# Moving five small norm tiles and 32 bytes in a 20,000-instruction transformer kernel, so that the big operands share one offset modulo 512 bytes

## The chip, the core and the metric

The kernel runs on one core of a Trainium2 chip. A core has TensorE (PE in the rows; PEld is its weight load), VectorE (DVE), ScalarE (ACT), GpSimd (POOL) and SyncE (SP, which issues most of the DMAs here). They share the on-chip memory SBUF, 128 partitions wide; TensorE writes its products into PSUM. Every tile below is 128 partitions high, and its address means the byte in each partition. The metric is the device time of one execution in microseconds (us); a time for a kernel is the median of several executions.

## What is computed

Two transformer blocks over 512 tokens of width 1024, in fp32. Cut to its skeleton:

```python
# first block (one layer)
x = x + rms_norm(hybrid_mixer(rms_norm(x), ...))            # sparse attention + matrix memory
x = x + rms_norm(memory_cross_attention(rms_norm(x), ...))
x = x + rms_norm((silu(h @ w_gate) * (h @ w_up)) @ w_down)  # h = rms_norm(x), d_ff 2816
# second block (two layers): half feed-forward, convolution module, half feed-forward,
# then half feed-forward, stick-breaking attention, half feed-forward
x = x + 0.5 * ((silu(h @ w_gate) * (h @ w_up)) @ w_down)    # four times
```

All norms are `x * rsqrt(mean(x*x) + eps) * gain`. Nearly all work is `activations @ weights`: five feed-forward modules of 1024 x 2816 x 3, and some twenty 1024-wide projections.

## The kernel before

Activations lie feature-major: a tile holds 128 features of all 512 tokens, 2 KB in each partition. fp32 accuracy comes from a split: `split` (lines 121 to 133) makes of a tile its rounded part `hi` (on ACT) and the remainder `lo` (on DVE), and `load_w` (line 159) does the same with a slab of weights, 128 x 1024, which SP's DMA queue has brought to `wraw`. `mm3` (lines 169 to 172) then adds three products, each a weight load and a matmul of 128 x 128 stationary by 128 x 512 moving:

```python
nc.tensor.matmul(ps, lh, rh, start=start, stop=False)   # L170: whi, xh
nc.tensor.matmul(ps, lh, rl, start=False, stop=False)   # L171: whi, xl
nc.tensor.matmul(ps, ll, rh, start=False, stop=stop)    # L172: wlo, xh
```

The stationary operand is a slice of 128 columns (512 bytes) of a weight slab, the moving one an activation tile. `projs` (line 195) walks the 8 K tiles of a projection, `ffn` (line 303) does each feed-forward module in two halves: in a half 11 F tiles, each a gate and an up projection from the activations `xh`, `xl` (11 x 2 x 24 = 528 matmuls), then 8 output tiles, each the down projection from the 11 tiles `hh`, `hl` (8 x 33 = 264 matmuls). `linear_out` (line 379) does an output projection from a module's result (`oh`, `ol` in the cross attention), and in the convolution module the second projection reads `ch`, `cl`, which have the tags and so the places of `xh`, `xl`. `token_tiles` (line 586) swaps the parts: there the activations are stationary and 256 columns of weights move.

The order on each engine comes from the framework's scheduler, except where a region is held in program order (`order_pe`). Weight slabs turn in three buffers of `wraw`, four of `whi` and four of `wlo`; a load waits for a free `wraw`, ACT's split for a free `whi`.

A norm takes the per-token sum of squares by matmuls with a column of ones, and then works on tiny tiles of 4 columns (16 bytes): `ms` (two buffers, line 257) and `rt` (three buffers, line 261), from which `rms_rows` (line 265) spreads the result over the partitions.

Where the tiles lie follows from the pools. Tiles of a pool stand one behind the other, each rounded up to 32 bytes, and the pools on the left side follow each other: `const`, `act_p`, `wp`, then those of the modules. `act_p` holds x, the 16 tiles `xh`, `xl`, four tiles for the squares, then the five small ones (5 x 32 = 160 bytes), then `rb`. In the program as built this gives:

```
tile                                  place                modulo 512
x, xh*, xl*, sq, sqacc, sqlast        from byte 20032          64
ms x2, rt x3                          77376 to 77535     (32 bytes each)
rb                                    77536                   224
wraw, whi, wlo                        from 81632              224
oh/ol, hh/hl, y, vsh, ksh             left side, later        224
cross attention qx*, k*               right side              224
cross attention pTh/pTl, vh/vl        right side              480
sparse attention kz, qn, P            right side               96
```

Of the kernel before, what the change touches and what calls it, by code (L numbers as in the profile page):

```python
# [14 lines left out]
P = 128  # L15
S = 512
# [32 lines left out]
def kernel(ctx: ExitStack, tc: tile.TileContext, t: dict, out: bass.AP):  # L49
# [34 lines left out]
    nhalf = const.tile([P, 4], F32, name="nhalf")  # L84
    nc.gpsimd.memset(nhalf, -0.5)
    nc.scalar.activation(const.tile([P, 4], F32, name="warm0"), nhalf, AF.Copy)
# [48 lines left out]
    # heads of 64: the exact product of queries and keys in two passes, (q_hi + q_lo) (k_hi + k_lo), with the  # L135
    # parts of the keys on the two halves of the partitions and each part of the queries on both
# [16 lines left out]
    def head_scores(ps, q, k, i):  # L153
        """scores of query tile i with its keys, the first 128 (i + 1)"""
        n = max((i + 1) * P, 256)
        for c in range(2):
            nc.tensor.matmul(ps[:, :n], q[c][:, i * P : (i + 1) * P], k[:, :n], start=c == 0, stop=c == 1)

    def load_w(ap, width, raw=None, pieces=1, hp=1):
        """a slab of weights as its rounded part and the remainder"""  # L160
        if raw is None:
            raw = wp.tile([P, width], F32, tag="wraw", bufs=3, name=nm("wraw"))
            nc.sync.dma_start(raw, ap)
        hi = wp.tile([P, width], F32R, tag="whi", bufs=4, name=nm("whi"))
        lo = wp.tile([P, width], F32R, tag="wlo", bufs=4, name=nm("wlo"))
        split(raw, hi, lo, pieces=pieces, hp=hp)
        return hi, lo
# [6 lines left out]
    # steps of a latency chain, put between the products of a run that TensorE takes in program order  # L174
# [27 lines left out]
    def square_acc(src, j, state, ts=WHOLE, apart=False, eng=nc.gpsimd):  # L202
        """adds a tile's squares to the running sum; the last tile's may stay apart"""
        if j == KT - 1 and apart:
            if "last" not in state:
                state["last"] = act_p.tile([P, S], F32, tag="sqlast", name=nm("sqlast"))
            nc.scalar.activation(state["last"][:, ts], src[:, ts], AF.Square)
            return
        sq = act_p.tile([P, S], F32, tag="sq", bufs=2, name=nm("sq"))
        nc.scalar.activation(sq[:, ts], src[:, ts], AF.Square)  # L210
        if j == 0:
            state["first"] = sq
        elif j == 1:
            state["acc"] = act_p.tile([P, S], F32, tag="sqacc", name=nm("sqacc"))
            eng.tensor_tensor(state["acc"][:, ts], state["first"][:, ts], sq[:, ts], ALU.add)  # L215
        else:
            eng.tensor_tensor(state["acc"][:, ts], state["acc"][:, ts], sq[:, ts], ALU.add)

    def inv_rms(state, eps=1e-6, ts=WHOLE, psum_only=False):
        """(mean of squares + eps)^-1/2 per token: as a column per token tile, and as a row on all partitions"""  # L220
        if not state:
            for j in range(KT):
                square_acc(x[j], j, state, eng=nc.vector)
        sums = rms_sums(state, eps, ts)
        rt, pb = rms_rows(sums, ts)
        if psum_only:
            return rt, pb
        rb = act_p.tile([P, S], F32, tag="rb", bufs=2, name=nm("rb"))[:, : ts.stop - ts.start]
        nc.vector.tensor_copy(rb, pb)
        return rt, rb  # L230

    def inv_rms_chain(state, first, second):
        """the steps of inv_rms, after that many products each; the result is there when they are done"""
        if not state:
            for j in range(KT):
                square_acc(x[j], j, state, eng=nc.vector)
        got = []

        def finish():
            rt, pb = rms_rows(got[0], WHOLE)  # L240
            rb = act_p.tile([P, S], F32, tag="rb", bufs=2, name=nm("rb"))
            nc.vector.tensor_copy(rb, pb)
            got[:] = [rt, rb]

        chain.append([first, lambda: got.append(rms_sums(state, 1e-6, WHOLE))])
        chain.append([second, finish])
        return got

    def rms_sums(state, eps, ts):
        n = (ts.stop - ts.start) // P  # L250
        pr = at_tile()
        accs = [state[k] for k in ("acc", "last") if k in state]
        for a, acc in enumerate(accs):
            for i in range(n):
                c = ts.start + i * P
                nc.tensor.matmul(pr[:, 4 * a + i : 4 * a + i + 1], acc[:, c : c + P], ones[:, 0:1], start=True, stop=True)
        ms = act_p.tile([P, 4], F32, tag="ms", bufs=2, name=nm("ms"))
        nc.vector.tensor_scalar(ms[:, :n], pr[:, :n], 1.0 / D, eps, ALU.mult, ALU.add)
        if len(accs) == 2:
            nc.vector.scalar_tensor_tensor(ms[:, :n], pr[:, 4 : 4 + n], 1.0 / D, ms[:, :n], ALU.mult, ALU.add)  # L260
        rt = act_p.tile([P, 4], F32, tag="rt", bufs=3, name=nm("rt"))
        nc.gpsimd.tensor_tensor(rt[:, :n], ms[:, :n], nhalf[:, :n], ALU.pow)
        return rt
# [14 lines left out]
    def post_norm_add(y, state, nxt):  # L278
        """x += y * rb, where y carries its gain already; a step for each half of the tokens"""
# [23 lines left out]
    def ffn(fp, xs, st, wg, wu, wd, out_cb, head=0, tail=0, step=None):  # L303
        """head: F tiles whose projections start with the first half of the tokens; tail: output tiles that end so"""
# [91 lines left out]
    # =====================================================================  # L396
    # hybrid mixer
    # =====================================================================
# [32 lines left out]
    # relative bias: u[h, i] = bias_h(511 - i), masked distances NEG; T[q, c] = -u[127 - q + c]  # L431
# [32 lines left out]
    # gate rows: 0..23 branch gates, 32..35 input gate, 64..67 forget gate  # L464
# [23 lines left out]
    # compressed keys and values  # L488
# [61 lines left out]
    # cumulative gates of the matrix-memory heads  # L550
# [28 lines left out]
    # branch gates, token-major  # L579
# [6 lines left out]
    def token_tiles(chunks, wd, xs_, ntok, cb, ws=None):  # L586
        """out[tokens, wd] for each token tile; chunks hold 1024 / wd K tiles of wd columns"""
# [26 lines left out]
    def coef(sums, h, br, floor):  # L614
        """gate over the sum of the exponentials, per token"""
# [7 lines left out]
    def softmax_rows(ps, bias, ptile, sm, masked):  # L623
        """ps holds the negated scores; writes exp(score - max) to ptile and its row sums to sm"""
# [165 lines left out]
    for hp in range(2):  # L790
# [19 lines left out]
        for i in range(NT):  # L810
# [12 lines left out]
            # num / d, normalized: num * (mean(num^2) + eps d^2)^-1/2 with d = max(|den|, exp(-m))  # L823
# [64 lines left out]
    # =====================================================================  # L888
    # memory cross attention
    # =====================================================================  # L890
# [87 lines left out]
    # P: projection of a feature tile, Q: its query, S, V: a head's scores and values  # L978
# [21 lines left out]
    # =====================================================================  # L1000
    # feed-forward of the first block
    # =====================================================================
# [18 lines left out]
    # =====================================================================  # L1021
    # second block
    # =====================================================================
# [26 lines left out]
    # Depthwise taps on TensorE: 32 channels x 4 taps fill the rows, a diagonal per tap the columns,  # L1050
    # and four such column tiles run side by side; the other taps run on VectorE.
# [45 lines left out]
    def depthwise(j, sets, gl, R, wbd, ts=WHOLE):  # L1097
# [6 lines left out]
        # two independent chains of multiply-adds on VectorE  # L1104
# [17 lines left out]
    def ln_sums(ts):  # L1122
        """mean and variance per token"""
# [31 lines left out]
    def ln_finish(n, lm, m2, ts):  # L1155
        """SiLU of the normalized tiles"""
# [108 lines left out]
    def stick_scores(q, k):  # L1265
        Ws = []
        for i in range(NT):
# [6 lines left out]
            # diagonal block: masked scores  # L1274
# [112 lines left out]
def _tile_cols(w):  # L1387
    """[K, N] -> [N / 128][128 rows of a K tile][K tile][128 columns]"""
# [4 lines left out]
def _tile_rows(w, per):  # L1393
    """[K, N] -> [chunk][128][per K tiles][N]"""
# [4 lines left out]
def _quarters(w):  # L1399
    """groups of 256 columns, each [chunk][128][4 K tiles][256]"""  # L1400
    return np.stack([_tile_rows(w[:, g : g + 256], 4) for g in range(0, w.shape[1], 256)])
# [111 lines left out]
```

## Time and profile before

| what | value |
|---|---|
| three executions | 2839.34 us median (2836.4 to 2841.1) |
| the profiled execution | span 2837.0 us from first to last instruction; its whole time is not listed apart |
| TensorE busy | 2777.5 us, 98% of the span |
| VectorE, ScalarE, GpSimd busy | 52%, 38%, 12% |
| DMA | 263.19 MB, mean 93 GB/s |
| granted TensorE clock | 0.991 of full speed, mean |

In the timeline a matmul's row gives its start and its duration; the durations overlap, since the next matmul enters while the last drains, so the distance from start to start is what a matmul costs TensorE. A form such as `128*128 128x512` is stationary size, then partitions and columns of the moving operand.

### The profile page before, as it was taken

The numbers are of one execution on the slowest core, as the hardware profiler recorded it, in microseconds if no ns is written. First come the engines' busy times: TensorE is split into PE (matmuls) and PEld (weight loads), VectorE is DVE, ScalarE is ACT, GpSimd is POOL, SyncE is SP. The second block draws the span as 40 slices with busy tenths as digits, with TensorE's granted clock in tenths as the row PEclk, the third lists the DMA queues.
The fourth block names the chain that finished last, engine by engine and source line by source line (L and its number), as shares of the span: only waits on it lengthen the run. The fifth ranks groups of instructions, "written<-read, shape, count | busy, mean of one in ns | idle before, by whom it ended". The sixth has DMA issues, their size and how long they took to land.

```text
span 2837.0 us, 35182 instructions
## 1 busy us (share of the span) xinstructions
PE 2777.5 (98%) x13750; PEld 2258.7 (80%) x13750; DVE 1465.4 (52%) x2270; ACT 1075.0 (38%) x1772; POOL 337.9 (12%) x451
## 2 busy tenths in 40 slices
PE   9999999999999999999899999999999997999998
PEld 6877988888888888885688888898888874788887
DVE  7666474643436434449754344434434489543443
ACT  6775544423234222332332233342222366322223
POOL 0133132100002000012210000100000136200001
PEclk9999999999999999999999999999999999999999
DMA  5213321223222232236232322322232310222322
GB/s 199 96 46 105 112 75 58 92 77 109 95 84 90 87 105 96 80 113 171 76 104 86 108 90 83 110 84 101 80 108 87 105 66 3 82 95 84 106 81 81
DMA packets 86923, 263.19 MB, mean 93 GB/s; under 512 B 9655, under 2 KB 13751, under 8 KB 86756
## 3 DMA queue, kind: packets, MB, share of 16 engines
q1 hardware_dynamic: 85148, 258.42, 27.7%
q10 hardware_dynamic: 1608, 2.52, 0.3%
q8 instruction: 108, 1.77, 0.2%
q14 instruction: 59, 0.48, 0.1%
HBM read 256.60 MB, written 4.30 MB: 92 GB/s over the span
## 4 chain that ended last, share of the span: by engine, by line
PE 79%; DVE 4%; DMA 1%; issue 1%; ACT 1%; POOL 0%; SPq 0%; DVEq 0%; ACTq 0%
PE sc L172 9%; PE sc L170 9%; PE sc L171 9%; PE mm L172 7%; PE mm L171 7%; PE mm L170 7%; PE tr L172 6%; PE tr L171 6%; PE tr L170 6%; PE po L172 3%; PE po L170 3%; PE po L171 3%; DVE rm L1280 1%; DVE wlo L130 1%; PE sc L1101 1%
## 5 line engine op out<-in xcount | busy, mean ns | idle before, releaser
L126 ACT ACTIVATE whi<-wraw 128x1024 fp32r<-128x1024 f32 (+3 forms) x518 | 492.2, 955 | 1327.0 <-PE sc L171 458.2
L130 DVE TENSOR_TENSOR wlo<-wraw,whi 128x1024 fp32r<-128x1024 f32 (+4 forms) x559 | 581.6, 1049 | 388.3 <-ACT whi L126 387.4
L170 PE MATMUL mm<-xh,whi 128*128 128x512 f32 (+1 forms) x760 | 291.5, 384 | 5.7 <-ACT whi L126 5.7
L171 PE MATMUL mm<-xl,whi 128*128 128x512 f32 (+1 forms) x760 | 290.5, 382 | 5.5 <-DVE xl L133 5.5
L172 PE MATMUL mm<-xh,wlo 128*128 128x512 f32 (+1 forms) x760 | 291.7, 384 | 0.0
L172 PE MATMUL sc<-xh,wlo 128*128 128x512 f32 (+1 forms) x696 | 274.4, 394 | 0.0
L170 PE MATMUL sc<-xh,whi 128*128 128x512 f32 (+1 forms) x696 | 273.3, 393 | 0.0
L171 PE MATMUL sc<-xl,whi 128*128 128x512 f32 (+1 forms) x696 | 272.6, 392 | 0.0
L171 PE MATMUL tr<-xl,whi 128*128 128x512 f32 (+1 forms) x592 | 226.0, 382 | 2.0 <-DVE xl L133 2.0
L172 PE MATMUL tr<-xh,wlo 128*128 128x512 f32 (+1 forms) x592 | 227.1, 384 | 0.0
L170 PE MATMUL tr<-xh,whi 128*128 128x512 f32 (+1 forms) x592 | 226.2, 382 | 0.0
L215 POOL TENSOR_TENSOR sqacc<-sq,sq 128x512 f32<-128x512 f32 (+1 forms) x11 | 16.4, 1487 | 1618.6 <-issue 915.6
L316 DVE TENSOR_TENSOR su<-sc,rb 128x512 f32<-128x512 f32 x80 | 55.2, 691 | 265.2 <-PE sc L172 265.2
L171 PEld LDWEIGHTS mm<-xl,whi 128*128 128x128 f32 x760 | 144.9, 191 | 35.8 <-DVE xl L133 6.9
L170 PEld LDWEIGHTS mm<-xh,whi 128*128 128x128 f32 x760 | 144.8, 191 | 35.3 <-ACT whi L126 5.7
L172 PEld LDWEIGHTS mm<-xh,wlo 128*128 128x128 f32 x760 | 145.3, 191 | 28.4 <-DVE wlo L130 0.3
L170 PEld LDWEIGHTS sc<-xh,whi 128*128 128x128 f32 x696 | 130.7, 188 | 33.5 <-issue 3.4
L171 PEld LDWEIGHTS sc<-xl,whi 128*128 128x128 f32 x696 | 130.7, 188 | 31.5
L172 PEld LDWEIGHTS sc<-xh,wlo 128*128 128x128 f32 x696 | 130.7, 188 | 30.4
L171 PEld LDWEIGHTS tr<-xl,whi 128*128 128x128 f32 x592 | 112.3, 190 | 26.1 <-DVE xl L133 2.2
L170 PE MATMUL sc<-hh,whi 128*128 128x512 f32 (+1 forms) x352 | 132.6, 377 | 0.0
L171 PE MATMUL sc<-hl,whi 128*128 128x512 f32 (+1 forms) x352 | 132.3, 376 | 0.0
(531 smaller groups left out, 5583.3 us busy)
## 6 DMA issues: line engine op xcount, KB each, us to landing
wraw<-wg SPq DMA_DIRECT2D x110, 512.0 KB, 3.5
wraw<-wu SPq DMA_DIRECT2D x110, 512.0 KB, 3.4
wraw<-wd SPq DMA_DIRECT2D x80, 384.0 KB, 3.0
wraw<-wd SPq DMA_DIRECT2D x80, 320.0 KB, 2.8
wraw<-w_pw SPq DMA_DIRECT2D x24, 512.0 KB, 3.6
wraw<-w_in_f SPq DMA_DIRECT2D x15, 512.0 KB, 4.3
R<-glscr SPq DMA_DIRECT2D x28, 264.0 KB, 5.5
x<-xT SPq DMA_DIRECT2D x16, 256.0 KB, 4.7
```

Of the source, the lines that this page charges most:

```text
L126: last_hi[0] = nc.scalar.activation(hi[:, sl], src[:, sl], AF.Copy)
L130: nc.vector.tensor_tensor(lo[:, sl], src[:, sl], f32(hi[:, sl]), ALU.subtract)
L170: nc.tensor.matmul(ps, lh, rh, start=start, stop=False)
L171: nc.tensor.matmul(ps, lh, rl, start=False, stop=False)
L172: nc.tensor.matmul(ps, ll, rh, start=False, stop=stop)
L215: eng.tensor_tensor(state["acc"][:, ts], state["first"][:, ts], sq[:, ts], ALU.add)
L316: nc.vector.tensor_tensor(su, pu, rb, ALU.mult)
L1101: nc.tensor.matmul(pc[32 * cg : 32 * cg + 32, ts], wbd[:, 4 * g + cg], R[:, cg, 4 * g + ts.start : 4 * g + ts.stop], start=g == 0, stop=g ...
L1280: nc.vector.tensor_tensor_scan(rm[:, :L][:, ::-1], ob[:, 1 : L + 1][:, ::-1], ob[:, 1 : L + 1][:, ::-1], 1.0, ALU.mult, ALU.bypass)
```

## The change

Beside comments and docstrings, which go (all lines from 87 on have moved by at most one), three tiles are touched. `ms` and `rt` are taken from the pool `const` in place of `act_p`, and the tile `warm0`, written once at the start, gets 16 columns in place of 4, of which the same 4 are written:

```diff
     nhalf = const.tile([P, 4], F32, name="nhalf")
     nc.gpsimd.memset(nhalf, -0.5)
-    nc.scalar.activation(const.tile([P, 4], F32, name="warm0"), nhalf, AF.Copy)
+    warm0 = const.tile([P, 16], F32, name="warm0")
+    nc.scalar.activation(warm0[:, :4], nhalf, AF.Copy)
...
-        ms = act_p.tile([P, 4], F32, tag="ms", bufs=2, name=nm("ms"))
+        ms = const.tile([P, 4], F32, tag="ms", bufs=2, name=nm("ms"))
...
-        rt = act_p.tile([P, 4], F32, tag="rt", bufs=3, name=nm("rt"))
+        rt = const.tile([P, 4], F32, tag="rt", bufs=3, name=nm("rt"))
```

`const` grows by 160 + 32 = 192 bytes and `act_p` shrinks by 160. No instruction is added, taken away or moved: on each of the five queues the same instructions stand in the same order and wait for the same semaphores. What differs is addresses:

```
tile                                  before, mod 512    after, mod 512
x, xh*, xl*, sq, sqacc, sqlast             64                256
rb, wraw, whi, wlo                        224                256
oh/ol, hh/hl, y, vsh, ksh                 224                256
pTh/pTl, vh/vl                            480                480
qx*, k* of the cross attention            224                224
kz, qn, P of the sparse attention          96                 96
```

So it is the operands of the projections and of the feed-forward modules that come to lie at one offset; the pools on the right side stay where they were.

## Rows read from the trace of the kernel before

**Rows 1.** Page: span, busy time by engine, chain by engine.
```profile
span 2837.0 us, 35182 instructions
PE 2777.5 (98%) x13750; PEld 2258.7 (80%) x13750; DVE 1465.4 (52%) x2270; ACT 1075.0 (38%) x1772; POOL 337.9 (12%) x451
...
PE 79%; DVE 4%; DMA 1%; issue 1%; ACT 1%; POOL 0%; SPq 0%; DVEq 0%; ACTq 0%
```

**Rows 2.** Two stretches: length, then PE, PEld, DVE, ACT, POOL, PEclk, DMA share, GB/s.
```profile
1263.00:1380.00 117.00, 110.71 (x689) 72.27 (x688) 107.27 (x146) 26.62 (x32) 28.71 (x23) 0.99 0.56 146
1380.00:2293.00 913.00, 907.92 (x4261) 749.03 (x4261) 414.04 (x550) 299.39 (x408) 46.36 (x40) 0.99 0.28 94
```

**Rows 3.** Waits: who waited for whom, us in total, times, longest.
```profile
ACT whi L126 <- PE sc L171: 458.2, 141, 8.2
...
SPq L163 <- DVE wlo L130: 2317.4, 481, 96.8
```

**Rows 4.** Timeline of PE: firsts of a down half, an up half, a down half.
```profile
2025.14 0.39 PE L170 MATMUL sc<-hh,whi 128*128 128x512 f32 x1
...
2085.02 0.40 PE L170 MATMUL mm<-xh,whi 128*128 128x512 f32 x1
...
2208.24 0.40 PE L170 MATMUL sc<-hh,whi 128*128 128x512 f32 x1
```

**Rows 5.** Timeline of PE, convolution module's second projection: two, six matmuls apart.
```profile
1420.42 0.39 PE L170 MATMUL sc<-ch,whi 128*128 128x512 f32 x1
...
1421.82 0.39 PE L170 MATMUL sc<-ch,whi 128*128 128x512 f32 x1
```

**Rows 6.** Timeline of PE, cross attention: output projection, and values three matmuls apart.
```profile
460.67 0.39 PE L170 MATMUL sc<-oh,whi 128*128 128x512 f32 x1
...
462.03 0.39 PE L171 MATMUL tr<-ol,whi 128*128 128x512 f32 x1
...
453.19 0.39 PE L171 MATMUL po<-pTl,vh 128*128 128x512 f32 x1
...
453.87 0.39 PE L171 MATMUL po<-pTl,vh 128*128 128x512 f32 x1
```

**Rows 7.** Groups by form: 128x512 products of L170 that read xh.
```profile
L170 PE MATMUL sc<-xh,whi 128*128 128x512 f32 x680 | 268.6, 395 | 0.0
...
L170 PE MATMUL mm<-xh,whi 128*128 128x512 f32 x648 | 257.8, 398 | 5.7 <-ACT whi L126 5.7
...
L170 PE MATMUL tr<-xh,whi 128*128 128x512 f32 x512 | 202.3, 395 | 0.0
...
L170 PE MATMUL po<-xh,whi 128*128 128x512 f32 x272 | 108.4, 399 | 0.5 <-ACT whi L126 0.5
```

**Rows 8.** Busy time of instructions that touch xl, three stretches (PE first).
```profile
100.00:370.00 270.00, 43.04 (x127) 24.51 (x128) 3.28 (x6) 0.99 0.24 81
...
1263.00:1380.00 117.00, 44.14 (x121) 22.70 (x121) 0.00 (x0) 0.99 0.56 146
...
2293.00:2425.00 132.00, 12.78 (x32) 6.04 (x32) 0.00 (x0) 0.97 0.06 21
```

**Rows 9.** Timeline of PE: 256-column products, first ones and what follows the last.
```profile
1855.04 0.28 PE L170 MATMUL tr<-whi,xh 128*128 128x256 f32 x1
...
1900.62 0.40 PE L170 MATMUL tr<-xh,whi 128*128 128x512 f32 x1
...
473.59 0.28 PE L170 MATMUL tr<-oh,whi 128*128 128x256 f32 x1
...
484.02 0.39 PE L256 MATMUL sc<-ones,sqacc 128*128 128x1 f32 x3
```

**Rows 10.** Timeline of PE just after a norm's latency chain.
```profile
391.45 0.63 PE L170 MATMUL po<-xh,whi 128*128 128x512 f32 x1
391.88 0.63 PE L171 MATMUL po<-xl,whi 128*128 128x512 f32 x1
392.30 0.63 PE L172 MATMUL po<-xh,wlo 128*128 128x512 f32 x1
```

**Rows 11.** Busy time in that stretch (PEclk third from the end).
```profile
391.40:392.80 1.40, 1.40 (x5) 1.06 (x4) 1.37 (x3) 0.09 (x1) 0.00 (x0) 0.50 0.75 243
```

## The prediction

> **What bounds the kernel now.** I read the page first: TensorE is busy 2777.5 of 2837.0 us and makes 79% of the chain that ended last [rows 1]. The busy time by stretches says where that holds: from 1380 to 2293 us PE is idle for 5 of 913 us, with DVE at 45%, ACT at 33% and DMA at 0.28; in the convolution stretch, 1263 to 1380, DVE is busy 107 of 117 us and PE is the one that waits [rows 2]. The waits agree: ACT's split of weights waits 458 us for products to give back a buffer of whi, and SP's loads wait 2317 us for a free wraw [rows 3]. So outside a few latency chains the weights stand ready, and a matmul that gets shorter shortens the kernel.
>
> The next view is the timeline of PE, read by starts. In the feed-forward module from 2025 to 2208 us no gap is left. The down half runs 264 products from 2025.14 to 2085.02, 59.88 us, that is 226.8 ns each; the up half behind it runs 528 from 2085.02 to 2208.24, 123.22 us, 233.4 ns each [rows 4]. Both are the same lines 170 to 172, the same form, full clock. What differs is where the moving operand lies: hh at 224 modulo 512, like the weights; xh at 64, while the weights are at 224. That could still be the module's other work, so I looked for the same routine on other tiles. The convolution's second projection moves ch, at 64: six products in 1.40 us, 233.3 ns [rows 5]. The output projection of the cross attention moves oh, at 224: six in 1.36 us, 226.7 ns. The attention's values move pTl at 480 against vh at 480: three in 0.68 us, 226.7 ns [rows 6]. Where the two operands agree modulo 256 a 512-column product costs 226.7, where they stand 160 bytes apart it costs 233.4. I take 6.55 ns as the difference.
>
> **The change, part by part.** No instruction, DMA or wait is added, removed or moved on any queue, so every term is a change in how long things take.
>
> Products that move xh or xl: from 64 against 224 to 256 against 256. The L170 groups count 680 + 648 + 512 + 272 = 2112 [rows 7]; L171 and L172 have as many each, 6336, and ch and cl add 4 tiles x 24 = 96. If equal offsets are what counts, 6432 x 6.55 ns = 42.1 us go.
>
> Not all of it is on the path. Products with xl are a third of all that read x; in the stretches where latency chains or DVE decide there are 127 + 121 + 32 = 280 of them [rows 8], so at most 840 products, 5.5 us. I count half as lost: 2.8 us. In the rest nothing is late next: a slab's 24 products take 5.44 in place of 5.60 us, and in [rows 2] neither DVE nor ACT reaches half of the stretch.
>
> Products of 256 columns: with x stationary and weights moving, 384 from 1855.04 to 1900.62, 118.7 ns each; oh at equal offsets, 87 from 473.59 to 484.02, 119.9 ns [rows 9]. Whatever they do moves some hundreds by 1.2 ns in either direction: nothing, within 1 us.
>
> Products that move hh: 224 against 224 becomes 256 against 256, 5 modules x 2 x 264 = 2640. No row shows two operands at 256; 224 and 480, the equal pairs that are there, are the same modulo 256. So both the 2640 and the level to which the 6432 fall need bounds. Above: 233.4 ns, the dearest pair seen. [...] I take 226.8, the nearest rows: equal offsets, same shape, same lines. [...]
>
> The small tiles: ms, rt and warm0 keep their instructions and sizes; only their place changes. DMA, ACT and DVE now write at 256 too; at the loads in [rows 2] a change of some per cent there stays behind PE.
>
> Sum against the profiled execution: 2837.0 - 42.1 + 2.8 = 2797.7 us of span. The median of the runs is 2.3 us above that span, so 2800.0.
>
> [...]
>
> **The rivals.**
> [...]
>
> Placement is not the cause. Then down halves are cheaper because, say, fewer other engines' accesses fall into them, and the time stays at 2839. For it: up and down halves do differ in what DVE and ACT do beside them. Against: ch and oh go through the same projection and still differ [rows 5, 6].
>
> The odd start of the moving tile is what makes 226.8 cheap. hh, oh and pTl all start 32 bytes past a multiple of 64, xh and ch at a multiple of 64. If that, not equality, decides, the change gives xh nothing and lifts hh to xh's price: 2640 x 6.55 ns = 17.3 us more, 2857. It ends slower as soon as the moving tile's own start counts at all and equality does not. For it: every pair in [rows 4 to 6] sorts by it as well. Against: it asks that the plainer address be the dearer one.
>
> **How the numbers follow.** Equal offsets, 226.8 for all: 0.64, its own range 2790 to 2812 (the lost part between nothing and 5.5 us, the level of 226.8 off by 1 ns, which is 9 us). Better than equality: 0.13, between 2739 and the first. No cause: 0.11, 2839. The odd start: 0.12, 2857. The range of 2760 to 2845 holds the first, the third and half of the second, 0.81. What a measurement can tell from no change is about 0.2%, 6 us. Faster 0.77, same 0.11, slower 0.12.
>
> **What would show it.** In the profile after, an up half of 528 products should last 119.8 us in place of 123.2 and start every 226.8 ns; ch's projection likewise; down halves should stay at 59.9 us, the pTl products, which don't move, at 226.7. The number of products and the waits should be as before, and the stretch from 1263 to 1380 should hardly shrink. Down halves at 61.6 us would prove the odd start, up halves at 123 us the case without a cause, any pitch below 224 ns the better one. If pitches fall as said and the span does not, the waits of PE would have grown, and I was wrong on what stands ready.

## The result, and the profile after

The changed kernel takes 2798.85 us, the median of four runs (2794.92 to 2801.32), against 2839.77 us for the kernel before (2836.4 to 2841.1, four runs): a ratio of 0.9854 (0.984 to 0.9868). It is faster by 40.9 us; 2800.0 was predicted. All lines from 87 on stand one lower, so `mm3` is L171 to L173.

The page of the profiled execution, which took 2799.96 us: span, busy time by engine, chain by engine.

```profile
span 2798.2 us, 35182 instructions
PE 2731.0 (98%) x13750; PEld 2252.2 (80%) x13750; DVE 1465.1 (52%) x2270; ACT 1074.5 (38%) x1772; POOL 339.0 (12%) x451
...
PE 79%; DVE 4%; issue 1%; DMA 1%; ACT 1%; POOL 0%; SPq 0%; DVEq 0%; ACTq 0%
```

Beside [rows 1]: as many instructions on each engine. PE's busy time fell by 46.5 us and that of its weight loads by 6.5; DVE, ACT and POOL are within 1.1 us. So no work went; the matmuls got shorter. PE's idle time, span less busy time, rose from 59.5 to 67.2 us: that is why 46.5 us less work gave 38.8 us less span. ACT still waits for PE, a little less than in [rows 3] (waits: who for whom, us in total, times, longest):

```profile
ACT whi L127 <- PE sc L172: 430.7, 138, 8.0
```

Then the timeline of PE at the places of [rows 4]: first products of a down half, the up half behind it, the next down half.

```profile
1997.07 0.39 PE L171 MATMUL sc<-hh,whi 128*128 128x512 f32 x1
...
2056.91 0.39 PE L171 MATMUL mm<-xh,whi 128*128 128x512 f32 x1
...
2176.59 0.39 PE L171 MATMUL sc<-hh,whi 128*128 128x512 f32 x1
```

The down half still takes 59.84 us, 226.7 ns a product. The up half takes 119.68 us for its 528 products, 226.7 ns in place of 233.4. The convolution's second projection answers to [rows 5]:

```profile
1402.72 0.40 PE L171 MATMUL sc<-ch,whi 128*128 128x512 f32 x1
...
1404.11 0.39 PE L171 MATMUL sc<-ch,whi 128*128 128x512 f32 x1
...
1424.51 0.39 PE L171 MATMUL tr<-xh,whi 128*128 128x512 f32 x1
```

Six products in 1.39 us here, where [rows 5] has 1.40: so short a piece does not show the gain. Over all 96, from 1402.72 to the product that follows the last at 1424.51, the mean is 227.0 ns. In the kernel before the same 96 took 22.40 us, 233.3 ns each (first, and what follows the last):

```profile
1419.02 0.40 PE L170 MATMUL sc<-ch,whi 128*128 128x512 f32 x1
...
1441.42 0.39 PE L170 MATMUL tr<-xh,whi 128*128 128x512 f32 x1
```

The values of the cross attention, for [rows 6]:

```profile
452.63 0.40 PE L172 MATMUL po<-pTl,vh 128*128 128x512 f32 x1
...
453.32 0.39 PE L172 MATMUL po<-pTl,vh 128*128 128x512 f32 x1
```

Three in 0.69 us: these products have not moved, yet over 38 of them the mean went from 229.2 to 231.3 ns. Last the 256-column run of [rows 9], 384 products:

```profile
1829.91 0.28 PE L171 MATMUL tr<-whi,xh 128*128 128x256 f32 x1
...
1875.98 0.40 PE L171 MATMUL tr<-xh,whi 128*128 128x512 f32 x1
```

46.07 us, 120.0 ns each, against 118.7: 0.5 us dearer.

Where the 38.8 us of span came from follows from the two traces laid side by side, product by product of the program. The lead is how much earlier the changed kernel starts a product, measured from each span's start; "by the count" is the number of 512-column products with `xh`, `xl`, `ch` or `cl` up to there, times 6.6 ns (6420 of the 6432 are counted). That price is an estimate, so the last column is one too.

```
place (us, before)   lead    by the count   short of it
        56          -1.65        1.11          2.76
       357          -1.43        2.63          4.06
       407           0.47        3.08          2.61
      1259          13.61       16.47          2.86
      1359          14.16       18.32          4.16
      1409          16.30       18.32          2.02
      2261          31.68       34.16          2.48
      2412          31.71       35.40          3.69
      2830          38.64       42.37          3.73
```

From 407 to 1259 us and from 1409 to 2261 the lead grows as the count says, to 0.5 us. The rest lies at the start, where executions of one kernel differ as well (below), and beside the chains and the convolution.

### The profile page after: what moved, and what is told of

Same layout as the page of the kernel before. It is cut to its first block, busy times and chain, and to the rows that moved or that the text cites. A ratio compares the mean times of both kernels' runs of the same rounds, so it can differ in the third digit from the quotient of the medians.

```text
span 2798.2 us, 35182 instructions
## 1 busy us (share of the span) xinstructions
PE 2731.0 (98%) x13750; PEld 2252.2 (80%) x13750; DVE 1465.1 (52%) x2270; ACT 1074.5 (38%) x1772; POOL 339.0 (12%) x451
## 4 chain that ended last, share of the span: by engine, by line
PE 79%; DVE 4%; issue 1%; DMA 1%; ACT 1%; POOL 0%; SPq 0%; DVEq 0%; ACTq 0%
PE sc L171 9%; PE sc L172 9%; PE sc L173 9%; PE mm L172 7%; PE mm L173 7%; PE mm L171 7%; PE tr L171 6%; PE tr L172 6%; PE tr L173 6%; PE po L171 3%; PE po L172 3%; PE po L173 3%; DVE wlo L131 1%; PE po L1311 1%; DVE c L1114 1%
## 5 line engine op out<-in xcount | busy, mean ns | idle before, releaser
L171 PE MATMUL mm<-xh,whi 128*128 128x512 f32 (+1 forms) x760 | 287.7, 379 | 6.3 <-ACT whi L127 5.9
L173 PE MATMUL mm<-xh,wlo 128*128 128x512 f32 (+1 forms) x760 | 286.4, 377 | 0.0
L171 PE MATMUL sc<-xh,whi 128*128 128x512 f32 (+1 forms) x696 | 270.1, 388 | 0.0
L173 PE MATMUL sc<-xh,wlo 128*128 128x512 f32 (+1 forms) x696 | 269.2, 387 | 0.0
L171 PE MATMUL tr<-xh,whi 128*128 128x512 f32 (+1 forms) x592 | 223.1, 377 | 0.0
L173 PE MATMUL tr<-xh,wlo 128*128 128x512 f32 (+1 forms) x592 | 222.9, 376 | 0.0
L171 PEld LDWEIGHTS mm<-xh,whi 128*128 128x128 f32 x760 | 144.3, 190 | 33.2 <-ACT whi L127 5.9
L173 PEld LDWEIGHTS mm<-xh,wlo 128*128 128x128 f32 x760 | 144.2, 190 | 25.1 <-DVE wlo L131 0.3
L171 PEld LDWEIGHTS sc<-xh,whi 128*128 128x128 f32 x696 | 130.7, 188 | 29.6 <-issue 2.5
L173 PEld LDWEIGHTS sc<-xh,wlo 128*128 128x128 f32 x696 | 130.7, 188 | 26.5
L171 PE MATMUL sc<-hh,whi 128*128 128x512 f32 (+1 forms) x352 | 132.6, 377 | 0.0
L173 PE MATMUL sc<-hh,wlo 128*128 128x512 f32 (+1 forms) x352 | 132.2, 376 | 0.0
```

## The experiments

The first four kernels were timed on one chip; the kernel before took 2840.72 us beside them (median of 13 runs, 2837.22 to 2844.25).

**Equality at another place, and the 32 bytes.** The small tiles move, `warm0` stays as it was; then x, the weights and the module tiles all lie at 224 modulo 512.

```diff
-    warm0 = const.tile([P, 16], F32, name="warm0")
+    warm0 = const.tile([P, 4], F32, name="warm0")
```

> Only the move of ms and rt, without the 32 bytes: x, xh, xl, rb, weights, hh and oh all lie at 224 modulo 512. Equality theory (a 512-column product costs 226.7 ns where moving and stationary operand agree modulo 256): 226.7 ns in up and down halves, up half 119.5 us, time within 3 us of the changed kernel, about 2799. Rival, absolute placement (a start at a multiple of 256 is what makes it cheap): up halves stay above 230 ns, time between 2817 and 2840. The 32 bytes are then what brought the gain.

Measured: 2800.85 us (2798.42 to 2802.3), ratio 0.986 (0.9845 to 0.9875). The timeline of PE, same three places:

```profile
1995.84 0.39 PE L171 MATMUL sc<-hh,whi 128*128 128x512 f32 x1
...
2055.68 0.39 PE L171 MATMUL mm<-xh,whi 128*128 128x512 f32 x1
...
2175.36 0.39 PE L171 MATMUL sc<-hh,whi 128*128 128x512 f32 x1
```

59.84 and 119.68 us, as at 256. A multiple of 256 brings nothing that shows beyond equality, and neither do the added 32 bytes.

**The 32 bytes alone.** `ms` and `rt` go back to `act_p`, the wider `warm0` stays: x lies at 96, the weights and `hh` at 256, 160 bytes apart as before the change.

```diff
-        ms = const.tile([P, 4], F32, tag="ms", bufs=2, name=nm("ms"))
+        ms = act_p.tile([P, 4], F32, tag="ms", bufs=2, name=nm("ms"))
...
-        rt = const.tile([P, 4], F32, tag="rt", bufs=3, name=nm("rt"))
+        rt = act_p.tile([P, 4], F32, tag="rt", bufs=3, name=nm("rt"))
```

> Only the 32 bytes, ms and rt back in act_p: x, xh, xl at 96, rb, weights, hh, oh at 256. Equality theory: products that move xh or xl are 160 bytes off again, 233.4 ns, up half 123.2 us, down half 59.8 us, time as before, about 2840. Rival, absolute placement of the stationary operand or of the weights' splitting: weights at 256 suffice, 226.7 ns everywhere, about 2799. Rival, odd start of the moving tile (96 is 32 past a multiple of 64): 226.7 for xh as well.

Measured: 2837.8 us (2833.89 to 2840.45, ten runs), ratio 0.9988 (0.9979 to 0.9998). The timeline of PE:

```profile
2023.35 0.39 PE L171 MATMUL sc<-hh,whi 128*128 128x512 f32 x1
...
2083.23 0.40 PE L171 MATMUL mm<-xh,whi 128*128 128x512 f32 x1
...
2206.44 0.40 PE L171 MATMUL sc<-hh,whi 128*128 128x512 f32 x1
```

Down 59.88 us, up 123.21 us: the gain needs the small tiles' move. Here the moving `xh` starts 32 bytes past a multiple of 64 and is dear, `hh` starts on a multiple of 256 and is cheap: the opposite of what the odd start would make. The 2.9 us by which this kernel lies under the one before are inside what the prediction counts as no change; nothing was found for them.

**Unequal in the down halves.** A pool of 160 bytes between the weights and the module pools puts `hh`, `oh` and their companions at 416; x and the weights stay at 256.

```diff
+    padp = ctx.enter_context(tc.tile_pool(name="padp", bufs=1))
+    pad = padp.tile([P, 40], F32, name="pad")
+    nc.gpsimd.memset(pad[:, :1], 0.0)
```

> The changed kernel with 160 unused bytes between the weights' pool and the modules' pools: xh, xl and weights stay at 256, hh, oh and the attention output lie at 416. Equality theory: down halves rise from 59.8 to 61.6 us (233.4 ns), up halves stay at 119.5 us; some 2640 + 300 products by 6.6 ns, 17 to 19 us more than the changed kernel, about 2817. Rival (the price is xh's own, bound to the up halves or to where x lies): down halves stay at 59.8 us and the time at 2799.

Measured: 2821.04 us (2819.17 to 2823.07), ratio 0.9934 (0.9918 to 0.9951). The timeline of PE:

```profile
2008.59 0.40 PE L174 MATMUL sc<-hh,whi 128*128 128x512 f32 x1
...
2070.44 0.39 PE L174 MATMUL mm<-xh,whi 128*128 128x512 f32 x1
...
2190.14 0.40 PE L174 MATMUL sc<-hh,whi 128*128 128x512 f32 x1
```

Now the down half is dear, 61.85 us or 234.3 ns a product, and the up half cheap, 119.70 us. The cost follows the distance, not the half. It came out 4 us above the expectation, since a product cost 7.6 ns more here and not 6.6. By the trace 2508 products of 512 columns move `hh` or `hl`, since some outputs are done in two halves of 256 columns (the expectation's 2640 takes all as whole): 2508 x 7.6 = 19.1 us of the 21.0 that lie between this and the next kernel.

**The changed kernel once more, beside them.**

> The changed kernel itself, on the same chip as the three others, as their yardstick: 226.7 ns in up and down halves, 2795 to 2802 us.

Measured: 2799.99 us (2797.32 to 2804.23), ratio 0.9859 (0.9844 to 0.9874), within 1 us of equality at 224.

**Other distances.** A pad at the head of the weight pool shifts weights, `hh` and `oh` together by 32, 64 or 128 bytes against x (the diff is for 32; the others have 16 and 32 columns).

```diff
+    pad = wp.tile([P, 8], F32, tag="pad", bufs=1, name="pad")
+    nc.gpsimd.memset(pad[:, :1], 0.0)
```

> The changed kernel with 32 unused bytes ahead of the weights' pool: xh, xl stay at 256, weights, hh and oh lie at 288; so only the products that move xh or xl have unequal operands, by 32 bytes. Equality modulo 256 in every byte: up halves 123.2 us (233 ns and more), down halves 59.8, about 2840. Rival, equality modulo 32 is enough: 119.5 us and 2799. Rival, the price grows with the distance: between 227 and 233 ns, 2805 to 2830.

> The same with 64 bytes: weights, hh and oh at 320, xh and xl at 256. Equality modulo 256: up halves about 123.2 us, about 2840. Rival, equality modulo 64: 119.5 us and 2799.

> The same with 128 bytes: weights, hh and oh at 384, xh and xl at 256. Equality modulo 256: up halves about 123.2 us, about 2840. Rival, equality modulo 128: 119.5 us and 2799. If the distance counts, this is the greatest there is and the dearest. A pitch below 226.7 would be a better place than the changed kernel's.

One run each: 2836.57, 2835.05 and 2834.95 us, the kernel before beside them 2835.45. An up half at 32 bytes of distance, 123.20 us, from its first product to the next down half's:

```profile
2081.17 0.40 PE L173 MATMUL mm<-xh,whi 128*128 128x512 f32 x1
...
2204.37 0.39 PE L173 MATMUL sc<-hh,whi 128*128 128x512 f32 x1
```

Up halves cost 233.34, 233.33 and 233.33 ns a product, down halves 226.8, 226.7 and 226.7. Even 32 bytes of distance take the whole gain away; from 32 to 128 bytes there is no slope.

**One slab in three.** 160 bytes between the buffers of `whi` and `wlo`: of the three products of `mm3` only L177's weights are off against x.

```diff
         hi = wp.tile([P, width], F32R, tag="whi", bufs=4, name=nm("whi"))
+        if not padded:
+            padded.append(wp.tile([P, 40], F32, tag="pad", bufs=1, name="pad"))
+            nc.gpsimd.memset(padded[0][:, :1], 0.0)
         lo = wp.tile([P, width], F32R, tag="wlo", bufs=4, name=nm("wlo"))
```

> The changed kernel with 160 unused bytes between whi and wlo: xh, xl and whi at 256, wlo, hh and oh at 416. It tells which weights a running product is measured against. Theory, those that are loaded for the next product while it runs: in an up half the product on line 172 and its successor's start (wlo is loaded meanwhile) is the dear one, one in three, 120.7 us; in a down half hh (416) runs while whi (256) is loaded in two of three, about 61.0 us. Rival, its own weights: in an up half the product with wlo, also one in three and 120.7 us; in a down half hh and hl against whi, two of three. The halves last the same in both, the starts tell: the distance from the xl product to the wlo product is the long one in the theory, that from the wlo product to the next whi product in the rival. Rival, no pairs at all: halves as in the changed kernel, 119.5 and 59.8 us.

Measured: 2842.9 us, one run. The timeline of PE (lines are four lower):

```profile
2025.88 0.40 PE L175 MATMUL sc<-hh,whi 128*128 128x512 f32 x1
...
2086.86 0.40 PE L175 MATMUL mm<-xh,whi 128*128 128x512 f32 x1
...
2210.06 0.40 PE L175 MATMUL sc<-hh,whi 128*128 128x512 f32 x1
```

The up half takes 123.20 us, as if every slab were off, where both the theory and its rival said 120.7. Nor is one start in three the dear one: the mean distances after a product of L175, L176 and L177 are 234.7, 233.7 and 231.7 ns. The down half, where two loads in three are off against `hh`, takes 60.98 us here and 60.7 to 61.0 in the eight halves of 264 products, 230.0 to 231.0 ns a product: near the 61.0 expected, and less than one load in three costs in the up half. So the sum over pairs fails for one in three and comes near for two. The next kernel has products without the network.

**Products alone.** 56 segments, mostly of 48 products, each with its own distance of moving and stationary start; the tile `X` starts at 128 modulo 512 and so does `W`, and "moving at 16" means 16 bytes on from there.

```python
def segment(ms, ss, n=S, cols=P, x=X, w=W, reps=48, size=4):
    for i in range(reps):
        m = ms[i % len(ms)] // size + (i % 3 * S if x is X else 0)
        s = ss[i % len(ss)] // size + (i % 6) * P
        nc.tensor.matmul(ps[:cols, :n], w[:, s : s + cols], x[:, m : m + n], start=i == 0, stop=i == reps - 1)
```

> Not the network: a kernel that loads x and one slab of weights once and then runs 56 segments of 48 products (the first of 96) with nothing else on any engine; its output is not the reference's. Each segment fixes where the moving and the stationary operand start: distances of 0 to 256 bytes in steps of 16, equal starts at seven places, segments in which one or two of three operands are 160 bytes off, 256 and 384 columns, 64 columns of weights, bf16. Theory, the two reads of PE itself get in each other's way unless they agree modulo 256: distance 0 and 256 cost 226.7 ns, all other multiples of 32 about 233 ns, equal starts 226.7 at every place; and one operand of three off costs as much as all, as the run before showed. Rival, the other engines' accesses are the partner: alone, all segments of fp32 cost the same, 227 ns or less. Rival, pair by pair: one of three off costs a third, about 229 ns. Open: steps of 16 bytes, bf16 (a rounded copy at half the bytes), fewer columns of weights.

Some stretches, each from the first product of a segment to the first of the next (stretch, its length, busy PE, granted clock, DMA): moving at 0 and weights at 0, 32 and 256; both at 16; weights one in three at 160; two of three at 160; moving at 160 and weights two of three at 0; bf16 with weights at 0 and 128. A segment issues 48 products; the count in brackets has a neighbour or two more.

```profile
36.57:47.45 10.88, 10.88 (x50) 1.00 0.00 0
...
58.34:69.53 11.19, 11.19 (x50) 1.00 0.01 1
...
214.40:225.28 10.88, 10.88 (x49) 1.00 0.00 0
258.84:270.03 11.19, 11.19 (x49) 1.00 0.01 1
...
324.63:335.82 11.19, 11.19 (x49) 1.00 0.01 1
...
335.82:346.92 11.10, 11.10 (x49) 1.00 0.00 0
...
380.48:391.52 11.04, 11.04 (x49) 1.00 0.01 1
...
548.00:558.37 10.37, 10.37 (x49) 1.00 0.00 0
...
579.09:589.45 10.36, 10.36 (x49) 1.00 0.01 2
```

Divided by 48: 226.7 ns for equal and for 256, 233.1 for 32, 233.1 for one in three, 216 for bf16 wherever the weights lie. Two loads in three off cost less than one: 231.3 with the moving tile at 0 (231.1 by the starts once settled), and 230.0 in the arrangement of the down half above, which so comes back without the network. The mean distance of the 7th to 42nd starts of segments:

```
moving at 0, weights at   0   16   32   48   64   80   96  112  128  144  160  176
ns                      226.7 226.7 233.3 233.3 233.3 232.0 234.3 233.3 233.3 233.3 233.3 230.0
weights at              192  208  224  240  256  288  384  480
ns                      228.9 233.3 233.3 226.7 226.7 233.3 232.4 233.3
both at                  16   32   64   96  160  224
ns                      233.3 226.9 226.8 226.8 227.3 227.3
256 columns, at 0, 32, 128, 160       120.0 118.2 118.8 120.0
384 columns, the same                 173.3 173.3 176.2 176.7
64 columns of weights, 0, 128, 160    230.0 229.4 230.0
bf16, at 0, 32, 64, 128, 160          215.9 215.9 215.8 215.8 215.8
```

No other engine has work in the fp32 segments of 128 x 128 by 512 but the last, next to no DMA is under way (2 GB/s at most in these rows), and the clock is at its full level (1.00): both prices come back, 226.7 and 233.3. So the price comes from where TensorE's two operands lie, and neither from the network nor from contention with other engines. Moving at 160 and weights at 0 cost 234.3, the price of the down halves at 416; the other way round it is 233.3. Where the weights lie against the moving tile decides 6.7 ns for these fp32 products, and for bf16 it decides nothing, 215.8 to 215.9 at the five distances tried.

**How odd loads add up.** The same kernel with other segments, most of 96 products. A load is called odd when its weights lie 160 bytes (or 32, where said) off the moving tile.

```python
segment([0], [0] * 5 + [160], reps=96)                                # one odd load in six
segment([0] * 6 + [160] * 6, [0] * 6 + [160] * 6, reps=96)            # a product's own two agree
segment([0] * 6 + [160] * 6, [160] + [0] * 6 + [160] * 5, reps=96)    # agrees with the next one's weights
```

> The kernel is replaced by 512-column products alone on an otherwise idle core; nothing of the network is computed. It asks why one slab of weights in three that lies 160 bytes off costs as much as all three. In the products alone that came before, odd weight loads gave a mean of 233.3 ns where one in three was odd, 230.2 where one in six was, against 226.67 with all equal and 233.33 with all off. Theory A: an odd load costs some 20 ns, but in the mean never more than 6.67 ns a product. One odd load in 2, 3, 4, 6, 12, 24 products: 233.3, 233.3, 231.7, 230.0, 228.3, 227.5 ns; blocks of 2, 3, 6, 11 odd loads in 12: 228.3, 228.3, 230.0, 232.8. Rival B: 6.67 ns for each odd load: 230.0, 228.9, 228.3, 227.8, 227.2, 226.9; blocks: 227.8, 228.3, 230.0, 232.8. Rival C: any odd load makes all of a sequence pay: 233.3 throughout. Odd by 32 should be as odd by 160. Which two operands count: moving tile and weights both change place every six products. If the moving tile must agree with the next product's weights, loaded beside it, the second arrangement is near 226.7 and the first, two unequal in twelve, about 230; if a product's own pair counts, the reverse. Blocks that never agree: 233.3. Starts that are no multiples of 32: moving at 0, weights at 4, 8, 248: near 226.7; moving at 16: 233.3 whatever the weights; moving at 4 or 8: open, 226.7 to 233.3.

Stretches of 96 products, one odd load in 3, 4, 6, 12 and 24, then all odd (busy PE, PEld, DVE, ACT, POOL, clock, DMA):

```profile
69.75:92.16 22.41, 22.41 (x98) 18.01 (x97) 0.00 (x0) 0.00 (x0) 0.00 (x0) 1.00 0.00 1
92.16:114.56 22.40, 22.40 (x98) 18.01 (x97) 0.00 (x0) 0.00 (x0) 0.00 (x0) 1.00 0.00 0
114.56:136.66 22.10, 22.10 (x98) 18.02 (x96) 0.00 (x0) 0.00 (x0) 0.00 (x0) 1.00 0.00 1
136.66:158.58 21.92, 21.92 (x98) 18.02 (x96) 0.00 (x0) 0.00 (x0) 0.00 (x0) 1.00 0.00 1
158.58:180.42 21.84, 21.84 (x98) 18.02 (x96) 0.00 (x0) 0.00 (x0) 0.00 (x0) 1.00 0.00 1
...
335.75:358.14 22.39, 22.39 (x97) 18.02 (x96) 0.00 (x0) 0.00 (x0) 0.00 (x0) 1.00 0.00 1
```

By the starts of the products, once settled, the means are 233.33, 233.33, 230.00, 228.33 and 227.50 ns, and 233.33. So one odd load costs (230.00 - 226.67) x 6 = 20.0 ns, and by the same working 19.9 ns where it is one in 12 or in 24. In the segment of one in twelve the distances read 237, 232, 231, 227: one odd load delays three products, by 10, 5 and 4 ns. One in three therefore already costs 20 / 3 = 6.7 ns a product, the price of all odd: theory A holds for 3, 6, 12 and 24, and the up half of the kernel with one slab off follows from it. By 32 bytes in place of 160 it is the same (233.33, 230.00, 228.33). Theory A missed at one in four (233.3, said 231.7), at one in two (231.7, said 233.3) and for blocks: two, three, six, eleven odd in twelve gave 230.0, 232.2, 231.7, 232.8. It also misses two odd loads in three, for which it gives 233.3 and the products alone 231.1 and 230.0. So 20 ns is the price of an odd load that stands alone; how several add up is open.

Which two operands must agree was not settled. A product's own pair gave 231.1 ns, agreement with the next one's weights 231.7, with those of the one before 231.1, never agreeing 233.9; none came near 226.7. The products alone have the same question with a change at every product: there a product's own pair gave 234.0 and agreement with the next one's weights 229.8, which speaks for the latter and is not borne out by the longer blocks. One moving tile in six at 160, with all weights at 0, costs 231.7, more than one odd load in six (230.0). Starts off the 32-byte grid went against the expectation: weights at 4, 8 and 248 with moving at 0 cost 232.4, 230.6 and 233.3, moving at 16 is cheap with weights at 32 or 48 (226.7) and dear with 0 and 16 (231.7, 233.3), moving at 4 costs 238.

No segment of 512 columns went under 226.67 ns with fp32 operands, so no placement that was tried has more to give.

## Why the prediction was right

**What bounds the kernel.** Right outside the convolution. Of the 42.4 us that the count gives, 38.8 left the span. The waits, said to stay as before, did not quite: PE's idle time grew by 7.7 us.

**The price of 6.55 ns.** Right: 233.4 fell to 226.7 in all up halves, and the convolution's second projection went from 233.3 to 227.0. The argument from `ch` against `oh`, the same lines with other addresses, was the one that carried; it rested on six products of each, and over whole runs it holds (before: 96 of `ch` and `cl` at 233.3 ns, 116 distances of `oh` and `ol` at 226.8). The experiment with the down halves at 416 turned the two prices round, 234.3 in the down half and 226.7 in the up half.

**The level to which they fall.** 226.8 was taken, with 233.4 as the bound above; it is 226.67 at 256 and at 224. The chances put 0.13 on better than equality, from 2739 us on. No run shows that time or a price that leads to it: no stretch or segment of fp32 products of 512 columns came out under 226.67 ns each. Three products start 0.43 and 0.42 us apart at a granted clock of 0.50 [rows 10, 11]; half of that, some 213 ns, is an estimate for the full clock that no fp32 run reached. Better than equality falls with the result itself, 226.7 ns in the up half, and with the first experiment, the same at 224; the odd start with the result, where `xh` starts on a multiple of 256 and is cheap (226.7), and with the second, where `hh` does so (226.8); that placement is not the cause with both, and with the products alone.

**hh at 256 against 256.** Nothing, as taken: 59.84 against 59.88 us. The 2640 products are 132 too many, as said with the down halves; the sum does not use it.

**The lost part.** 2.8 us said, 3.7 by the lead table, but in other places. The convolution stretch, which "should hardly shrink", shrank by 2.7 us from 1259 to 1409 us, more than its count of 1.9. The timeline of PE there, first the kernel before (first product with `R` of the convolution, first of its second kind), then the changed one:

```profile
1278.74 4.50 PE L1101 MATMUL sc<-R,wbd 128*32 128x512 f32 x40
...
1377.25 1.07 PE L1101 MATMUL po<-R,wbd 128*32 128x256 f32 x16
```

```profile
1264.63 4.50 PE L1102 MATMUL sc<-R,wbd 128*32 128x512 f32 x40
...
1360.98 1.29 PE L1102 MATMUL po<-R,wbd 128*32 128x256 f32 x20
```

98.5 us became 96.4. It would be wrong to put these 2.2 us down to shorter products. In the kernel with the 32 bytes alone, where `xh` is as dear as before, the same stretch took 95.3 us:

```profile
1280.16 4.50 PE L1102 MATMUL sc<-R,wbd 128*32 128x512 f32 x40
...
1375.45 2.37 PE L1102 MATMUL po<-R,wbd 128*32 128x256 f32 x40
```

Over all traces it took 95.3 to 98.7 us with dear `xh` and 95.8 to 96.5 with cheap, so what sets it is open. DVE's 107 of 117 busy microseconds [rows 2] were read as PE waiting there; the same row has PE busy for 110.7, so it did not show that. In 2293 to 2425 the gain was indeed lost, 1.2 us. The largest piece, 2.8 us by 56 us, was not foreseen: the first 48 products took until 21.3 us, against 19.0 before. In the same kernel run again they took until 19.4, and with all at 224 until 18.5, so this is the start's scatter and no cost of the change. That the sum met the measured time to 1.2 us is therefore in part luck: such scatter, and the convolution's, is larger.

**256 columns.** Dearer by 1.3 ns at equal offsets, which was inside the 1 us allowed. The products alone show the same reversal (120.0 equal, 118.2 at 32).

**pTl.** Said to stay at 226.7. The mean went from 229.2 to 231.3, and is 229.4 with all at 224. The 226.7 was read from three products [rows 6], which is too few here. Their operands did not move, so neighbours may count, as they do for an odd load (three products delayed, above); that is not shown: with the down halves at 416, where x and the weights lie at 256 as well, the mean is 229.8. It concerns some 40 products.

**What the prediction did not see** is how the cost adds up. It priced each product by its own pair, and that held because the change brings both slabs to x's offset at once. Had `wlo` stayed off, the same arithmetic would have kept two thirds of the gain in the up halves, where the run shows none; with two loads in three off the products alone show 231.1 and 230.0 ns, about what the arithmetic gives (231.1).

## What to carry to other kernels

Where TensorE bounds a kernel and streams fp32 products of 128 x 128 by 512, list the start address modulo 256 of every moving and stationary tile and make them one, in steps of 32 bytes (226.7 against 233.4 ns a product in the up halves here); a few small tiles between two pools are enough to spoil it, here by 1.5%. Make all of them agree: one weight load in three left off cost as much as all (233.3 ns), two in three somewhat less (231.1 and 230.0). To find such a thing, take one line of code that runs on different tiles and compare distances from start to start, not durations or busy shares, over whole stretches.

## What the runs showed of the hardware

- 128 x 128 by 512 in fp32, full clock: 226.67 to 227.3 ns a product with operands equal modulo 256 on the 32-byte grid, 232.0 to 234.3 at other distances from 32 to 224 bytes (176 and 192 lie lower, 230.0 and 228.9), on an otherwise idle core too; bf16 215.8 to 215.9 at the five distances tried.
- One weight load in 6, 12 or 24 that lies 160 bytes off costs about 20 ns, in 6 or 12 by 32 bytes as well, and at one in 12 it is spread over three products (10, 5 and 4 ns); one in three costs as much as all (233.3), two in three less (230.0 and 231.1).
- At 256 columns equal offsets are no gain (120.0 against 118.2 at 32), and with 64 columns of weights every distance costs 229.4 to 230.0 ns.
- Between equal offsets and bf16 there remain 10.8 ns a product (226.67 against 215.8 to 215.9) for which no run shows a reason; neither does any show why distance matters, or which two operands have to agree.
